# A decoder layer on one core: x's blocks summed on chip, low parts and scalings moved by a step, the gates started earlier

## The chip, the core and the metric

The kernel runs on one core of one Trainium2 chip. The metric is the device time of one execution in microseconds (us). A core has these engines, each with a queue of its own that it works off in order: TensorE (PE, matmuls; PEld is its weight load), VectorE (DVE), ScalarE (ACT), GpSimd (POOL) and SyncE (SP, which issues most DMAs). DMAs are issued from the queues of SP, ACT and POOL. An instruction that waits for a semaphore holds everything behind it on its engine.

## The reference, cut to what matters

```python
xn = rmsnorm(h, g_mix)                                   # x: 512 x 2048, float32
q_a, k_c, v_c, k_s, v_s, k_w, v_w, g_nsa, c_q, c_kv, k_r, gate_a, gate_b = split(xn @ w_in)
o_a = nsa_attention(...)                                 # compressed, selected and window branches
o_b = mla_attention(...)                                 # 16 heads, low-rank keys and values
mixed = sigmoid(gate_a) * (o_a @ w_o_nsa) + sigmoid(gate_b) * (o_b @ w_o_mla)
h = h + mixed @ w_out
h = h + memory_cross_attention(rmsnorm(h, g_xattn), rmsnorm(mem, g_mem), ...)   # 256 tokens of memory
h = h + square(relu(rmsnorm(h, g_mlp) @ w_ff1)) @ w_ff2
return rmsnorm(h, g_final)
```

All arrays are float32. There is one layer, a sequence of 512, a width of 2048, and an MLP of 8192.

## The kernel before, in words

**Matmuls in two parts.** Every operand of a matmul is split into a high part, rounded to the type that PE takes at full rate (ACT writes it: `copy` or `activation` with a scale), and a low part, the difference (DVE writes it: `tensor_sub`, or `scalar_tensor_tensor` with a scale). A product is three matmuls: high times high, high times low, low times high (`mm`, L516 to L518, for the attention's side; L2086 to L2088 for gates and MLP). `split` (L526 to L533) writes both parts at once. `split_late` (L546, L547 or L549, L550) writes the high part and puts the low part on a list that is worked off one or two runs later.

**Order of the work.** The schedule is written out by hand. A stage is a loop over chunks of columns; in a chunk, k runs over the blocks of 128 input features, and in each k the four blocks of 128 tokens (tt) get their three matmuls. Between the matmuls of a chunk other work is dealt out: weights (`Stream`: loads by SP at L320, high parts at L335, low parts at L347; the raw areas are two, and a load waits for the low part of the unit that lay in its area), attention (`side`, one piece at a time, at a rate given for each stage), and one background generator, `self.bg`, that is advanced once or four times per k (`bgn`). `on_k(k)` is called ahead of the matmuls of a k. PSUM banks come from rings: four `mm`, three `st` and one `o`; a transpose into `st` waits for the readers of the bank three allocations ago.

**Stages.** Seven projection chunks `P` (0 to 6) of xn @ w_in without its gates; two chunks `M` for MLA's low-rank inputs; memory's keys (`mem_k`) and values (`mem_v`) beside NSA's attention; for each quarter of MLA's heads its queries, keys and values (`mla_q`, `mla_kv`) and then a chunk `wn` of o_a @ w_o_nsa; the gates (`Gates.run`); the mix (`mix`, chunks `wm`); w_out; cross attention; the MLP.

**Seven products for eight.** Gates, w_out and MLP work on two-by-two blocks with seven block products, whose operands are sums of blocks. For the gates the blocks of x, scaled by g_mix, are `d_x[t, h, i]` in DRAM (t half of the tokens, h half of the features, i half of that half; 512 KB each), and the sums are `d_s[n, i]`, n from 1 to 4. `x_blocks` (L938 to L972) makes both. It starts at k = 13 of chunk 0 with four loads of x from DRAM (L947, SP), goes on as background in chunk 1, four steps per k, scales the four areas of 128 x 1024 in 16 steps on ACT (L960), stores them (L961), makes four sums on DVE (L968) and stores each (L969); then the same for i = 1, whose loads are issued ahead of the sums of i = 0. Sums 3 and 4 are written over the areas A[1, 1] and A[0, 1]. The same chunk 1 holds, from k = 4 on, `proj_post(0)`: rotations on POOL (`rope`, L635 to L638, after L1053 on DVE), then `to_compress` for each tt: four transposes into an `st` bank (L1112), two into another (L1120), copies by ACT (L1114, L1122) and low parts by DVE (L1115, L1123).

**Memory.** `mem_load` loads the 8 parts of mem, and in 16 steps splits them (ACT L532, DVE L533), squares and adds them (ACT L624, POOL L625). A step is taken in each k of chunk `M` 1, and then in each k under 15 of `mem_k(0)`; the rest is drained at k = 12. `mem_scale` multiplies memory's keys by their row's norm (a broadcast by two matmuls, ACT copy, DVE product L1733 of 128 x 1024) and scales the values (ACT L1736, two of 128 x 512). It stands between `mla_kv(2)` and chunk `wn` 1.

**Heads' rows.** `load_o` reads the eight stored pairs of heads back from DRAM and splits them (ACT L529, DVE L530), one per step, three steps after its load; once for NSA (in MLA's second quarter) and once for MLA (in the gates).

**Start of the gates.** In the last chunk `wn` 3 (8 values of k) the gates get ready. The generator `fetch` (four loads from d_x and d_s: L2326, L2331) runs as background: its first step does nothing, the second issues the loads, at k = 1. At k = 5 come four loads of weights (`loads(4)`, L1885), at k = 6 and 7 `ahead(0)` and `ahead(1)`. `ahead(s)` casts one half of the first moving operand (`stat`, ACT L1976), writes the low part of the half before (`stat_low`, DVE L1981), and calls `prep(s)`: high parts of weights up to s + 1 (ACT L1897), low parts up to s (DVE L1902), loads up to s + 4. Loads of the second and later products add the new weights to an area in place (POOL, L1892), so each waits for the two parts made of what lay in it. `Gates.run` then calls, for each product p and each j of 0 to 3, `prep(4p + j + 3)`, `stat` or `stat_low` for the next product, and the matmuls; at its very start it also calls `stat_low(0, 1)`.

## Time and profile before

| | |
|---|---|
| median of 3 runs | 2803.4 us (2802.63 to 2807.19) |
| profiled execution, its own time | 2804.49 us |
| its span | 2802.7 us |
| granted clock of PE, mean | 0.996 |
| DVE, ACT, POOL busy | 72%, 59%, 17% of the span |
| read from HBM, written | 460.84 MB, 50.33 MB |
| chunk P 0, P 1 (x's blocks) | about 5 to 50 us, 50 to 101 us |
| chunk M 1 (memory's loading), mem_k(0) | about 494 to 546 us, 546 to 560 us |
| chunk wn 3, gates | about 829 to 858 us, 858 to 1175 us |

The time of a kernel is taken in several executions; the profile is one more, with its own time. Its span runs from the first to the last instruction. In a row of the timeline stand the start (us), the duration (us), engine and line, operation, what it writes and reads with shapes, the count where several were merged, and in brackets the idle time of the engine just before it and what ended that. In the list of waits stand who waited for whom, us in total, times, and the longest. PE's matmuls overlap: a row's duration is longer than the distance to the next.

### The profile page before, as it was taken

How to read it: one execution, taken by the hardware profiler on the slowest of the kernel's cores; microseconds unless marked ns; L12 is line 12 of the kernel's file. 1: busy time of each engine (PE TensorE's matmuls, PEld its weight loads, DVE VectorE, ACT ScalarE, POOL GpSimd, SP SyncE). 2: the span in 40 equal slices, each digit the busy share in tenths (PEclk: the TensorE clock that was granted, in tenths of full speed). 3: DMA queues.
4: the chain of work that ended last, by engine and by line, in shares of the span. 5: the costliest groups of instructions: out<-in, count | busy, mean ns of one | idle time of the engine just before them, and what ended most of it. 6: DMA issues, size and time to landing. Idle time of an engine off the chain costs nothing.

```text
span 2802.7 us, 38326 instructions
## 1 busy us (share of the span) xinstructions
PE 2766.2 (99%) x13974; PEld 2354.6 (84%) x13974; DVE 2022.5 (72%) x3195; ACT 1645.5 (59%) x2746; POOL 467.6 (17%) x690
## 2 busy tenths in 40 slices
PE   9899999999999999999999999999999999999998
PEld 8788889888887788889998888888888888888887
DVE  6547766777666777657775877777777778888788
ACT  6435555776665666534566766766666644444445
POOL 3111111211111111101220111111111111111110
PEclk9999999999999999999999999999999999999999
DMA  7531111223338998879644988889888989889996
GB/s 247 196 97 59 67 56 65 95 100 106 106 136 225 259 232 188 265 263 228 154 95 152 241 207 208 204 221 216 210 216 200 235 225 228 225 227 235 239 232 174
DMA packets 171726, 513.69 MB, mean 183 GB/s; under 512 B 17552, under 2 KB 38928, under 8 KB 171536
## 3 DMA queue, kind: packets, MB, share of 16 engines
q0 software_dynamic: 50688, 184.57, 34.8%
q1 hardware_dynamic: 96064, 295.56, 30.0%
q10 hardware_dynamic: 24784, 31.11, 3.2%
q8 instruction: 109, 1.79, 0.3%
q14 instruction: 81, 0.66, 0.1%
HBM read 460.84 MB, written 50.33 MB: 182 GB/s over the span
## 4 chain that ended last, share of the span: by engine, by line
PE 81%; DMA 5%; DVE 5%; ACT 3%; issue 3%; POOL 1%; SPq 0%; DVEq 0%; POOLq 0%; ACTq 0%
PE mm L2087 10%; PE mm L2086 10%; PE mm L2088 10%; PE mm L516 7%; PE mm L517 7%; PE mm L518 7%; PE st L2086 5%; PE st L2088 5%; PE st L2087 5%; DMA s<-wts 4%; PE st L801 2%; PE o L820 1%; PE st L516 1%; PE mm L1656 1%; PE mm L1658 1%
## 5 line engine op out<-in xcount | busy, mean ns | idle before, releaser
L2086 PE MATMUL mm<-s,s 128*128 128x512 f32 x1472 | 575.0, 391 | 2.9 <-ACT s L2434 2.1
L2087 PE MATMUL mm<-s,s 128*128 128x512 f32 x1472 | 573.0, 389 | 0.1
L2088 PE MATMUL mm<-s,s 128*128 128x512 f32 x1472 | 572.9, 389 | 0.0
L1902 DVE TENSOR_TENSOR s<-s,s 128x1024 fp32r<-128x1024 f32 x307 | 372.7, 1222 | 201.2 <-ACT s L1897 200.4
L1897 ACT CAST s<-s 128x1024 fp32r<-128x1024 f32 x307 | 318.1, 1049 | 207.9 <-DMA s<-wts 160.1
L516 PE MATMUL mm<-s,s 128*128 128x512 f32 (+5 forms) x1044 | 411.7, 394 | 1.9 <-DVE s L1524 0.7
L518 PE MATMUL mm<-s,s 128*128 128x512 f32 (+5 forms) x1044 | 394.9, 378 | 0.2 <-DVE s L533 0.2
L517 PE MATMUL mm<-s,s 128*128 128x512 f32 (+5 forms) x1044 | 394.5, 378 | 0.0
L347 DVE TENSOR_TENSOR s<-s,s 128x512 fp32r<-128x512 f32 (+4 forms) x408 | 286.3, 717 | 90.1 <-ACT s L335 89.5
L335 ACT CAST s<-s 128x512 fp32r<-128x512 f32 (+4 forms) x408 | 242.1, 604 | 158.6 <-DMA s<-wts 81.9
L2086 PEld LDWEIGHTS mm<-s,s 128*128 128x128 f32 x1472 | 276.6, 188 | 60.7 <-ACT s L2434 2.5
L2088 PEld LDWEIGHTS mm<-s,s 128*128 128x128 f32 x1472 | 276.6, 188 | 57.5
L2087 PEld LDWEIGHTS mm<-s,s 128*128 128x128 f32 x1472 | 276.7, 188 | 56.9 <-DVE s L1902 0.5
L1897 ACT CAST s<-d 128x1024 fp32r<-128x1024 f32 x168 | 174.5, 1048 | 175.5 <-DMA d<-wts 148.6
L2086 PE MATMUL st<-s,s 128*128 128x512 f32 x676 | 264.2, 391 | 0.0
L2088 PE MATMUL st<-s,s 128*128 128x512 f32 x676 | 262.8, 389 | 0.0
L2087 PE MATMUL st<-s,s 128*128 128x512 f32 x676 | 262.5, 388 | 0.0
L1892 POOL DMA_DIRECT2D s<-wts x160 | 139.8, 876 | 714.1 <-DVE s L1902 330.5
L1902 DVE TENSOR_TENSOR s<-d,s 128x1024 fp32r<-128x1024 f32 x168 | 204.3, 1221 | 70.2 <-ACT s L1897 69.8
L518 PEld LDWEIGHTS mm<-s,s 128*128 128x128 f32 x1044 | 196.6, 188 | 34.5 <-DVE s L533 1.0
L704 ACT ACTIVATE PP<-PP,mx 128x512 f32<-128x512 f32 (+2 forms) x208 | 116.3, 559 | 184.7 <-DVE mx L703 184.2
L516 PEld LDWEIGHTS mm<-s,s 128*128 128x128 f32 x1044 | 197.3, 189 | 25.3 <-DVE d L1369 1.2
(393 smaller groups left out, 5090.8 us busy)
## 6 DMA issues: line engine op xcount, KB each, us to landing
s<-wts SPq DMA_DIRECT2D x278, 512.0 KB, 5.4
s<-wts POOLq DMA_DIRECT2D x192, 512.0 KB, 8.6
d<-wts POOLq DMA_DIRECT2D x108, 512.0 KB, 8.6
d<-wts SPq DMA_DIRECT2D x60, 512.0 KB, 8.1
PP<-wts POOLq DMA_DIRECT2D x52, 512.0 KB, 8.5
PP<-wts SPq DMA_DIRECT2D x33, 512.0 KB, 8.1
d_u<-s ACTq DMA_DIRECT2D x64, 256.0 KB, 5.3
d<-d_u SPq DMA_DIRECT2D x19, 512.0 KB, 8.4
```

The source lines that it names most:

```text
L335: self.k.nc.scalar.copy(o.hr, self.at[n][:, s])
L347: self.k.nc.vector.tensor_sub(o.lr, t[:, s], o.hi)
L516: t.matmul(ps, a.hr, b.hr, start=first, stop=False)
L517: t.matmul(ps, a.hr, b.lr, start=False, stop=False)
L518: t.matmul(ps, a.lr, b.hr, start=False, stop=last)
L704: self.later("x", 1, lambda: nc.scalar.activation(p, p, AF.Exp, bias=mx, scale=-1.0, accum_out=sm))
L1892: self.nc.gpsimd.dma_start(t, src, accum_op=OP.add)
L1897: self.nc.scalar.copy(t.hr, self.raw[i])
L1902: self.nc.vector.tensor_sub(t.lr, r, t.hi)
L2086: m(ps, a.hr, b.hr, start=first, stop=False, skip_group_check=True)
L2087: m(ps, a.hr, b.lr, start=False, stop=False, skip_group_check=True)
L2088: m(ps, a.lr, b.hr, start=False, stop=last, skip_group_check=True)
```

## The change

- `x_blocks` no longer loads x. The blocks are put together on DVE from the two parts that chunk 0 left on chip (`self.X[k]`, high + low, already scaled by g_mix): 32 additions of 128 x 256, two in a step. It starts with chunk 1. The block d_x[1, 0, i], which nothing reads, is not stored. The sums come in the order 1, 4, 2, 3, three steps apart instead of two; sum 4 is written over A[1, 0] instead of A[0, 1].
- `mem_load` writes a part's low part at the start of its next step, and `mem_k(0)` takes a step of it in every third k instead of every k.
- `load_o` likewise writes each low part a step later.
- `mem_scale` becomes a generator that is advanced once per k in the chunks of the mix, so it runs in k = 1 to 4 of the first of them.
- Start of the gates: `fetch` at k = 0, the four loads of weights at k = 1 (before: 5), `stat(0, 0)` at 3, `prep(0)` at 4, `stat_low(0, 0)` and `stat(0, 1)` at 5, `prep(1)` at 6, `stat_low(0, 1)` and `prep(2)` at 7 of chunk `wn` 3; `Gates.run` no longer begins with `stat_low(0, 1)`.

```diff
     def x_blocks(self):
         nc, v = self.nc, self.nc.vector
-
-        def load(i):
-            A = {}
+        for i in range(2):
+            A = {(t, h): self.slots.get() for h in range(2) for t in range(2)}
             for h in range(2):
-                for t in range(2):
-                    d = 8 * h + 4 * i
-                    A[t, h] = self.slots.get()
-                    nc.sync.dma_start(A[t, h].rearrange("p (k n) -> p k n", k=4),
-                                      self.a["xT"][d:d + 4, :, 256 * t:256 * t + 256].rearrange("k p n -> p k n"))
-            return A
-
-        A = load(0)
-        for i in range(2):
-            if i == 0:
-                yield
-            for h in range(2):
-                for t in range(2):
-                    for kk in range(4):
-                        yield
-                        x, d = A[t, h][:, 256 * kk:256 * kk + 256], G_MIX + 8 * h + 4 * i + kk
-                        nc.scalar.activation(x, x, AF.Copy, scale=self.gains[:, d:d + 1])
+                for kk in range(4):
+                    yield
+                    x = self.X[8 * h + 4 * i + kk]
+                    for t in range(2):
+                        s = slice(256 * t, 256 * t + 256)
+                        v.tensor_add(A[t, h][:, 256 * kk:256 * kk + 256], x.hi[:, s], x.lo[:, s])
+                for t in range(1 + h):
                     nc.sync.dma_start(self.d_x[t, h, i], A[t, h])
-            B = load(1) if i == 0 else None
             S = [self.slots.get(), self.slots.get()]
-            for n, o, f, a, b in ((1, S[0], v.tensor_sub, A[1, 0], A[1, 1]), (2, S[1], v.tensor_sub, S[0], A[0, 0]),
-                                  (3, A[1, 1], v.tensor_add, S[1], A[0, 1]), (4, A[0, 1], v.tensor_sub, A[0, 0], A[1, 0])):
+            for n, o, f, a, b in ((1, S[0], v.tensor_sub, A[1, 0], A[1, 1]), (4, A[1, 0], v.tensor_sub, A[0, 0], A[1, 0]),
+                                  (2, S[1], v.tensor_sub, S[0], A[0, 0]), (3, A[1, 1], v.tensor_add, S[1], A[0, 1])):
                 yield
                 yield
                 f(o, a, b)
                 nc.sync.dma_start(self.d_s[n, i], o)
+                yield
             yield
             self.put(*S, *A.values())
-            A = B
...
             if k == 8:
                 self.late_loads()
-            elif k == 13:
-                self.bg = self.x_blocks()
-                next(self.bg)
-                self.bg, self.xb = None, self.bg
...
-                self.bg, self.bgn = self.xb, 4
+                self.bg, self.bgn = self.x_blocks(), 4
...
-            if q == 2:
-                self.mem_scale()
             self.wn(q - 1, T["rw"], rows if q == 1 else None)
...
         g = Gates(self)
-        self.bg = g.fetch()
 
         def on_k(k):
             if k:
                 self.put(self.N[k - 1])
-            if k == 5:
-                drain(self.bg)
-                g.loads(4)
             if k == 6:
                 self.W.trim()
-            if k > 5:
-                g.ahead(k - 6)
-
+            steps[k]()
+
+        steps = [g.fetch, lambda: g.loads(4), lambda: None, lambda: g.stat(0, 0), lambda: g.prep(0),
+                 lambda: g.ahead(1), lambda: g.prep(1), lambda: (g.stat_low(0, 1), g.prep(2))]
         self.wn(3, T["rw"], on_k)
...
     def load_o(self, dram, out, lag=3):
...
-        for j in range(8 + lag):
+        low = None
+        for j in range(9 + lag):
+            if low:
+                h, x = low
+                self.nc.vector.tensor_sub(h.lr, x, h.hi)
+                out.append(h)
             if j < 8:
...
-            if j >= lag:
+            if lag <= j < 8 + lag:
                 while not self.slots.free:
                     yield
-                out.append(self.slot_hl())
-                self.split(out[-1], st[(j - lag) % 4])
-            yield
+                low = self.slot_hl(), st[(j - lag) % 4]
+                self.nc.scalar.copy(low[0].hr, low[1])
+                yield
+            elif j < lag:
+                yield
...
     def mix(self):
...
+        scale = self.mem_scale()
...
             def on_k(k):
+                next(scale, None)
...
     def mem_load(self):
...
-                self.split(h, x, self.gains[:, G_MEM + k:G_MEM + k + 1])
+                nc.scalar.activation(h.hr, x, AF.Copy, scale=g)
                 self.sumsq(x, k, sq[:, e * 256:e * 256 + 256], self.macc)
+                yield
+                nc.vector.scalar_tensor_tensor(h.lr, x, g, h.hi, op0=OP.mult, op1=OP.subtract)
                 self.MX.append(h)
-                yield
...
         def on0(k):
-            if k < 15:
+            if k % 3 == 0:
                 next(self.ml, None)
...
     def mem_scale(self):
         nc = self.nc
+        yield
         t = self.slots.get()
         rbm = t[:, :256]
         self.bcast(self.rm, rbm, 2)
+        yield
         k = self.kf.rearrange("p (h m) -> p h m", h=4)
         nc.vector.tensor_mul(k, k, rbm[:, None, :].to_broadcast([128, 4, 256]))
+        self.put(t)
         for i in range(2):
+            yield
             v = self.vf[:, i * 512:i * 512 + 512]
             nc.scalar.activation(v, v, AF.Copy, scale=self.rm[:, i:i + 1])
-        self.put(t)
...
     def ahead(self, step):
-        if step:
-            self.stat_low(0, step - 1)
+        self.stat_low(0, step - 1)
         self.stat(0, step)
-        self.prep(step)
...
-                if p == j == 0:
-                    self.stat_low(0, 1)
```

More of the change, by code (lines that the diff above doesn't have):

```diff
@@ L1446, in on_k @@
                 self.put(self.N[k - 1])
-            if k == 5:
-                drain(self.bg)
-                g.loads(4)
             if k == 6:
                 self.W.trim()
-            if k > 5:
-                g.ahead(k - 6)
+            steps[k]()
+        steps = [g.fetch, lambda: g.loads(4), lambda: None, lambda: g.stat(0, 0), lambda: g.prep(0),
+                 lambda: g.ahead(1), lambda: g.prep(1), lambda: (g.stat_low(0, 1), g.prep(2))]
         self.wn(3, T["rw"], on_k)
         self.put(self.N[-1])
-        self.bg = None
         return g
@@ L1684, in mem_load @@
                 k, x, s = 2 * j + e, st[j % 4][:, 256 * e:256 * e + 256], t[:, 512 * e:512 * e + 512]
-                h = HL(s[:, :256], s[:, 256:])
-                self.split(h, x, self.gains[:, G_MEM + k:G_MEM + k + 1])
+                h, g = HL(s[:, :256], s[:, 256:]), self.gains[:, G_MEM + k:G_MEM + k + 1]
+                nc.scalar.activation(h.hr, x, AF.Copy, scale=g)
                 self.sumsq(x, k, sq[:, e * 256:e * 256 + 256], self.macc)
+                yield
+                nc.vector.scalar_tensor_tensor(h.lr, x, g, h.hi, op0=OP.mult, op1=OP.subtract)
                 self.MX.append(h)
-                yield
         self.put(*sl[:2])
@@ L2318, in fetch @@
         self.A = {}
-        yield
         self.half(0, 0)
```

## Prediction

> **What bounds the kernel now.** I read the page first, then the list of waits of PE, then the timeline of every engine around each long wait, and at last a table of windows for the granted clock.
>
> ```profile
> PE 2766.2 (99%) x13974; PEld 2354.6 (84%) x13974; DVE 2022.5 (72%) x3195; ACT 1645.5 (59%) x2746; POOL 467.6 (17%) x690
> ```
>
> PE is busy for 2766.2 of 2802.7 us, so no edit that leaves the matmuls alone can bring more than the 36.5 us that are left, and what slow stretches hide inside the busy time. The other engines matter only where PE waits for them. The waits of PE, in us in total, times and longest:
>
> ```profile
> PE st L1120 <- DVE kc L1115: 6.4, 1, 6.4
> PE st L516 <- DVE s L547: 4.6, 5, 1.7
> PE o L822 <- DVE s L547: 4.2, 3, 2.4
> PE st L1300 <- DVE s L547: 2.4, 1, 2.4
> PE mm L2086 <- ACT s L2434: 2.1, 1, 2.1
> ```
>
> These five lines hold 19.7 us. Asked by stretches, the list puts them at 78 to 85 us (projection), 500 to 575 (memory's loading), 685 and 731 (MLA), 864 to 867 (start of the gates) and 955 (gates). From 1300 to 2750 us PE has no wait over 0.4 us, so that the MLP, half of the span, can only lose. The windows (PE, PEld, DVE, ACT and POOL busy us with instructions, granted clock, DMA share, GB/s) show what a wait costs beyond itself:
>
> ```profile
> 50.00:78.30 28.30, 28.30 (x148) 25.40 (x147) 12.59 (x21) 15.90 (x35) 8.72 (x17) 1.00 0.83 293
> 78.30:84.90 6.60, 0.20 (x2) 0.00 (x0) 1.09 (x2) 4.29 (x10) 0.00 (x0) 0.80 0.77 309
> 85.00:89.00 4.00, 4.00 (x12) 3.45 (x13) 2.90 (x5) 3.83 (x8) 0.00 (x0) 0.50 0.33 131
> 502.40:505.10 2.70, 0.33 (x3) 0.07 (x2) 1.08 (x3) 1.89 (x6) 0.67 (x1) 1.00 0.00 0
> 505.50:508.90 3.40, 3.40 (x16) 3.17 (x15) 2.85 (x9) 3.40 (x10) 0.47 (x1) 0.51 0.02 5
> 867.30:870.70 3.40, 3.20 (x9) 2.09 (x9) 0.00 (x0) 0.70 (x1) 0.47 (x1) 0.51 1.07 265
> 954.90:957.40 2.50, 0.40 (x2) 0.00 (x0) 1.54 (x2) 2.50 (x4) 0.86 (x1) 1.00 1.07 211
> ```
>
> After three of the stops (6.6, 2.7 and about 2.7 us) the clock was granted at half for some 3.4 us or more with PE back at work; after the fourth (2.1 us of idle) it stayed at 1.00. Half speed over 4 us loses 2.0 us, over 3.4 us up to 1.7. The Trainium skill (TensorE: Matmul & The Clock Gate, "HAM oscillation") says to avoid PE-idle gaps above about 3.4 us. Here a gap of 2.7 us was enough, and the row decides; by the page the two shorter stops would be worth their idle time alone.
>
> **Stage 1: x's blocks (second projection chunk).** Rows of ACT, DVE:
>
> ```profile
> 80.61 0.58 ACT L335 CAST s<-s 128x464 fp32r<-128x464 f32 x1 [7.04 <-DMA s<-wts]
> 81.10 1.70 ACT L960 ACTIVATE s<-s,gains 128x256 f32<-128x256 f32 x4
> 82.70 1.04 ACT L1114 CAST kc<-st 96x512 fp32r<-96x512 f32 x1
> 83.78 1.08 DVE L1115 TENSOR_TENSOR kc<-st,kc 96x512 fp32r<-96x512 f32 x1 [9.34 <-ACT kc L1114]
> 68.58 1.23 DVE L968 TENSOR_TENSOR s<-s,s 128x1024 f32<-128x1024 f32 x1 [1.18 <-DMA d_x<-s]
> 56.76 0.18 DVE L598 RECIPROCAL rs<-rs 128x4 f32<-128x4 f32 x1 [2.48 <-ACT rs L595]
> ```
>
> ACT stood 7.04 us on a load of weights; behind it in its queue lay four scalings (L960) and the first copy of the compression (L1114), whose PSUM bank PE wanted at 78.3. The weights were late for two reasons: DVE, whose low parts free their raw areas, had stood on a store of x (L968, because block sum 3 and 4 write over areas still being stored), and the DMA engines were at 0.83 with eight 512 KB loads of x among the traffic. The change removes these eight loads, two of eight stores, all 32 scalings on ACT, and the wait of sum 4; sum 3 comes eleven steps after its store instead of six. So the wait for weights should go. What is late next is DVE: the 32 additions are now its work. By 78.3 it must have done its 12.6 us of before, two more sums (six instead of four have been issued by then, 2.5 us), the copy's low part (1.1 us), and the additions. No row shows such an addition. The nearest is the 256-wide low part L533, with ACT's and POOL's beside it:
>
> ```profile
> 502.68 0.46 ACT L546 CAST s<-st 128x384 fp32r<-128x384 f32 x1
> 504.02 0.48 DVE L533 SCALAR_TENSOR_TENSOR s<-s,gains,s 128x256 fp32r<-128x256 f32 x1 [2.10 <-ACT s L532]
> 504.42 0.55 DVE L547 TENSOR_TENSOR s<-st,s 128x384 fp32r<-128x384 f32 x1
> 508.43 0.73 POOL L625 TENSOR_TENSOR s<-s 128x256 f32<-128x256 f32 x1 [3.27 <-ACT s L624]
> 508.49 0.95 DVE L533 SCALAR_TENSOR_TENSOR s<-s,gains,s 128x256 fp32r<-128x256 f32 x1
> ```
>
> It takes 0.48 us and lets the next one start after 0.40; beside POOL's L625 it took 0.95. At 0.40, 32 additions are 12.8 us. The sum is 12.6 + 2.5 + 1.1 + 12.8 = 29.0, and DVE's wait for the square root (2.5) stays: 31.5 us in a stretch of 28.3. DVE comes 3.2 us late, PE waits that long, and half a clock for 3.4 us adds up to 1.7: 4.9 us. Before, it was 6.4 + 2.0 = 8.4. **Term 1: -3.5 us.** Bounds: a quarter of L968's 1.23 for an addition (0.31) leaves DVE 0.3 late, -8.1; 0.95 for the sixteen additions of the second half, which run beside POOL's rotations (POOL was busy 8.7 of the 28.3 us), puts 8.8 us on top, +5.3. I take 0.40 since POOL is idle in the first half.
> The Trainium skill (SBUF — State Buffer, "Who interferes with whom") speaks against the move: a DVE instruction with two SBUF inputs and a GpSimd instruction that reads SBUF exclude each other, and ACT never waits for either. The pair 0.48 and 0.95 agrees; by that rule alone the stage would give the +5.3 of the first rival below.
>
> **Stage 2: low parts of memory.** At 502 DVE waited 2.10 us for ACT's high part of memory, with L547 behind it, ready since 503.1 (502.68 + 0.46), and PE behind that. With the low part of the step before in its place, L547 starts 1.3 us sooner; PE's 2.4 becomes 1.1, short of what halved the clock, which gives up to 1.7 more (I take 1.2: 16 matmuls passed in the 3.4 us). Two more places:
>
> ```profile
> 539.10 0.48 DVE L533 SCALAR_TENSOR_TENSOR s<-s,gains,s 128x256 fp32r<-128x256 f32 x1 [0.89 <-ACT s L532]
> 551.60 0.48 DVE L533 SCALAR_TENSOR_TENSOR s<-s,gains,s 128x256 fp32r<-128x256 f32 x1 [1.43 <-ACT s L532]
> 552.68 0.49 DVE L533 SCALAR_TENSOR_TENSOR s<-s,gains,s 128x256 fp32r<-128x256 f32 x1 [0.59 <-ACT s L532]
> ```
>
> The first is worth 0.9. At 551 three steps of the loader came in a row within the first three k-steps; with one in three the last of them is no longer in front of L547, 1.1. **Term 2: -4.5 us** (bounds -2 and -7). The steps still end at k = 9, before k = 15 needs the last part. The heads' rows have the same form, with DVE waits but only small ones of PE near: **-0.4** (0 to -1).
>
> **Stage 3: scaling of memory's keys and values.**
>
> ```profile
> 728.66 1.21 DVE L1733 TENSOR_TENSOR s<-s,s 128x1024 f32<-128x1024 f32 x1
> 731.00 0.38 PE L516 MATMUL st<-s,s 96*128 96x256 f32 x1 [1.01 <-DVE s L547]
> 1193.31 0.69 DVE L347 TENSOR_TENSOR s<-s,s 128x512 fp32r<-128x512 f32 x1 [2.07 <-ACT s L335]
> ```
>
> L1733 stood before L547, and PE waited 1.01 us. In its new place, the first chunk of the mix, its two small matmuls, ACT copies and DVE product (1.21) stand before gate work; DVE waits 2.07 us there for ACT, which covers it. Without that cover it costs 1.2. **Term 3: -1.0 us** (+0.2 to -1.0).
>
> **Stage 4: start of the gates.**
>
> ```profile
> 828.09 2.37 SPq L1885 DMA_DIRECT2D s<-wts  x4
> 849.94 1.04 ACT L1976 CAST s<-s 128x1024 fp32r<-128x1024 f32 x1
> 855.80 1.05 ACT L1976 CAST s<-s 128x1024 fp32r<-128x1024 f32 x1
> 857.20 1.22 DVE L1981 TENSOR_TENSOR s<-s,s 128x1024 fp32r<-128x1024 f32 x1
> ...
> 866.51 0.56 DVE L547 TENSOR_TENSOR s<-st,s 128x384 fp32r<-128x384 f32 x1
> 867.12 0.33 PE L822 MATMUL o<-s,d 128*128 128x128 f32 x1 [2.40 <-DVE s L547]
> 860.20 0.87 POOL L1892 DMA_DIRECT2D s<-wts  x1 [5.11 <-ACT s L1399]
> 870.00 1.04 ACT L1897 CAST s<-s 128x1024 fp32r<-128x1024 f32 x1 [6.19 <-DMA s<-wts]
> 871.47 0.44 PE L820 MATMUL o<-s,d 128*128 128x384 f32 x1 [0.97 <-ACT s L546]
> ```
>
> The first loads went out at 828.09, 22 us before the first cast: SP had run ahead, so moving them five steps earlier is worth nothing by itself and passes nothing on SP that waits. What counts are the casts. Seven low parts of 1.1 us stand on DVE between 857.20 and 866.51 before the L547 that PE waits for; four of them move into k-steps 5 to 7 of the chunk before, where L547 comes some 4.5 us sooner, before PE asks. The adding load of 860.20 took 9.8 us and held ACT 6.19 us; its low part moves one step ahead (steps are about 5 us here, 849.94 to 855.80), so it lands near 865 and holds ACT for about 1. Gone are 2.4, the half clock (1.0 for the five matmul gaps in it) and most of 0.97 plus what ACT adds there: **term 4: -4.4 us** (0 to -6). The stop at 955 comes under a DMA share of 1.07; PE arrives some 4 us sooner and three loads start about as much sooner: 0 (-2 to +2).
>
> **Sum:** -3.5 - 4.5 - 0.4 - 1.0 - 4.4 = -13.8. The profiled execution took 2804.5 us, so 2790.7; the median of the runs, 2803.4, lies 1.1 below it: **2789.6 us**.
>
> **Rivals.** (1) DVE becomes the bound of the second projection chunk: the additions exclude POOL's rotations; term 1 is +5.3. For: 0.95 beside POOL. Against: POOL is idle for two thirds of the stretch. -13.8 + 8.8 = -5.0: 2798.4. (2) The gates start no sooner, since the DMA engines (1.07) and not the casts set their pace and the stop at 955 takes up what 864 gives: term 4 is 0, or the edit does not do what it says, as its loads were early already. 2794.0. (3) Slower: in k-steps 3 to 7 of the chunk before the gates, six casts of 1.05 us now stand on ACT before the attention's copies, and wait for slots that PE has just read or for loads not landed; each such stop is a 2.4 us wait plus half a clock, 3.5 us. Term 4 gone (-9.4), five of the six blocked give +8: 2811.5. It decides from three blocked casts on. Against: ACT is not the last one before 857 in any wait of PE there.
>
> **How the numbers follow.** 0.2% (5.6 us) is about what a measurement of this kernel can tell. Forecast 0.62; rival 1 0.17, half of it on either side of -5.6; rival 2 0.13; both together (-0.6) 0.04; rival 3 0.04. Faster: 0.62 + 0.07 + 0.12 = 0.81; same 0.10 + 0.01 + 0.04 = 0.15; slower 0.04. The range goes from 2780 (term 1 at -8.1, terms 2 and 4 near their better bounds) to 2799.5, which takes in rivals 1 and 2.
>
> **What would show it.** PE's wait on L1115 gone or down to some 3 us, with DVE and not ACT as the late one (its row without a long idle time before it); no half clock at 505 and 868; DVE's wait for L532 gone from the list; no L1733 near 729; ACT's 6.19 us under 2. I am wrong if the wait on L1115 is as long as before, or if new waits stand between 829 and 858.

## The result, and the profile after

The changed kernel takes 2789.1 us (median of 4 runs, 2787.53 to 2790.86); the kernel before, on the same chip, 2804.9 us (4 runs, 2802.63 to 2807.19). The ratio is 0.9944, with a 95% interval of 0.9927 to 0.9961: faster by 15.8 us by the medians. The profiled execution took 2789.5 us with a span of 2787.7 us, 15.0 less than before. The prediction was 2789.6 us, within 2780 to 2799.5.

From the page of the changed kernel, PE's line, and the two queues of DMA that carry most (packets, MB, the time of their packets as a share of 16 engines' span):

```profile
PE 2762.4 (99%) x13974; PEld 2351.7 (84%) x13974; DVE 2033.4 (73%) x3227; ACT 1633.1 (59%) x2714; POOL 469.7 (17%) x690
...
q0 software_dynamic: 50688, 184.57, 35.1%
q1 hardware_dynamic: 91552, 290.32, 29.9%
```

PE still has 13974 matmuls, so the n-th of one trace can be set against the n-th of another, once the four that `mem_scale` takes to its new place (from 726 to 1163 us) are left out. PE's longest waits in the changed kernel:

```profile
PE mm L2077 <- ACT s L2420: 3.4, 1, 3.4
PE st L516 <- DVE s L547: 2.4, 5, 1.0
PE o L822 <- DVE s L547: 2.2, 3, 1.4
PE st L1104 <- DVE kc L1099: 1.6, 1, 1.6
```

Line numbers have moved: L1104 and L1099 are L1120 and L1115 of before, L2077 is L2086, L2420 (tanh of the gates) is L2434. The wait of 6.4 us in the second projection chunk is 1.6; the 2.4 us of memory's loading (L1300 on L547) is off the list; the 2.4 us at the start of the gates (L822) is 1.4. One wait has grown: the stop in the gates from 2.1 to 3.4 us. The windows (PE, PEld, DVE, ACT, POOL busy us with instructions, granted clock, DMA share, GB/s) at these places:

```profile
50.00:78.50 28.50, 28.50 (x147) 25.59 (x146) 25.29 (x56) 10.15 (x18) 8.24 (x12) 1.00 0.66 243
78.50:80.80 2.30, 0.69 (x6) 0.43 (x5) 2.27 (x3) 1.08 (x1) 2.14 (x5) 1.00 1.05 344
80.80:84.80 4.00, 3.88 (x22) 3.28 (x23) 3.92 (x5) 0.85 (x2) 0.21 (x2) 1.00 0.95 306
851.00:854.00 3.00, 1.65 (x12) 1.38 (x11) 2.97 (x6) 0.96 (x3) 0.87 (x1) 1.00 1.01 304
937.60:941.40 3.80, 0.38 (x2) 0.00 (x0) 1.53 (x2) 2.60 (x4) 0.86 (x1) 1.00 1.07 251
941.50:944.50 3.00, 3.00 (x7) 2.37 (x8) 1.62 (x2) 1.50 (x2) 0.89 (x1) 0.50 1.06 210
```

In the first stretch (50.00 to 78.30 before) DVE has gone from 12.59 to 25.29 us and ACT from 15.90 to 10.15. After the stop at 78.5 and the one at 851 the clock stays at 1.00, where before it was halved. After the stop at 937.6 it is halved, which before it was not.

Where the 14.4 us between the first and the last matmul came from: take the start of the same matmul in both traces, and ask how much their difference grows over a stretch. For example PE's row of the transposes at L1112 and the next at L1120 stood at 77.91 and 84.92 before; after (L1096, L1104) they stand at 78.51 and 80.71, so 7.01 us have become 2.20. In us, by the changed kernel's times, "before" less "after":

| stretch of the changed kernel | 0 to 45 | 45 to 120 | 120 to 490 | 490 to 600 | 600 to 760 | 760 to 846 | 846 to 880 | 880 to 920 | 920 to 946 | 946 to 1150 | 1150 to 1300 | to the end |
|---|---|---|---|---|---|---|---|---|---|---|---|---|
| what is there | chunk 0 | x's blocks | | memory | MLA, scaling | | gates' start | | gates' stop | | mix | |
| won | -0.6 | 7.0 | -0.1 | 4.2 | 1.8 | 0.7 | 4.2 | 0.2 | -2.9 | 0.0 | -0.1 | 0.2 |

### The profile page after: what moved, and what is told of

Its sections match the earlier page's. It is cut to its first block, busy times and chain, and to the rows that moved or that the text cites. A ratio compares the mean times of both kernels' runs of the same rounds, so it can differ in the third digit from the quotient of the medians.

```text
span 2787.7 us, 38302 instructions
## 1 busy us (share of the span) xinstructions
PE 2762.4 (99%) x13974; PEld 2351.7 (84%) x13974; DVE 2033.4 (73%) x3227; ACT 1633.1 (59%) x2714; POOL 469.7 (17%) x690
## 3 DMA queue, kind: packets, MB, share of 16 engines
q0 software_dynamic: 50688, 184.57, 35.1%
q1 hardware_dynamic: 91552, 290.32, 29.9%
## 4 chain that ended last, share of the span: by engine, by line
PE 83%; DMA 6%; DVE 5%; ACT 3%; issue 2%; SPq 0%; POOL 0%; DVEq 0%; POOLq 0%; ACTq 0%
PE mm L2077 10%; PE mm L2079 10%; PE mm L2078 10%; PE mm L516 7%; PE mm L518 7%; PE mm L517 7%; PE st L2079 5%; PE st L2077 5%; PE st L2078 5%; DMA s<-wts 2%; PE st L801 2%; DMA PP<-wts 1%; PE st L516 1%; PE st L518 1%; PE o L820 1%
## 5 line engine op out<-in xcount | busy, mean ns | idle before, releaser
L2077 PE MATMUL mm<-s,s 128*128 128x512 f32 x1472 | 575.0, 391 | 3.6 <-ACT s L2420 3.4
L2077 PEld LDWEIGHTS mm<-s,s 128*128 128x128 f32 x1472 | 276.7, 188 | 61.1 <-ACT s L2420 3.9
L2077 PE MATMUL st<-s,s 128*128 128x512 f32 x676 | 264.2, 391 | 0.0
```

Of the source, the lines that this page charges most:

```text
L2077: m(ps, a.hr, b.hr, start=first, stop=False, skip_group_check=True)
```

## The experiments

Each was timed in turn with the kernel before, which took 2803.3 us beside e1 to e4 and 2804.6 to 2804.9 beside the others and the change. The change itself was not timed again beside them. The first five take one part of the change away, or make it alone.

| run | median, us | ratio to before | 95% interval |
|---|---|---|---|
| the change | 2789.1 | 0.9944 | 0.9927 to 0.9961 |
| e1_old_xblocks | 2795.0 | 0.9972 | 0.9961 to 0.9982 |
| e2_old_memory | 2793.2 | 0.9959 | 0.9947 to 0.9972 |
| e3_old_gates_start | 2792.8 | 0.9962 | 0.9950 to 0.9975 |
| e4_old_scale | 2789.5 | 0.9951 | 0.9937 to 0.9965 |
| e5_only_xblocks | 2797.3 | 0.9973 | 0.9962 to 0.9983 |
| e6_sums_early | 2786.8 | 0.9936 | 0.9923 to 0.9948 |
| e7_pool_adds | 2789.7 | 0.9945 | 0.9932 to 0.9957 |
| e8_late_loads | 2787.2 | 0.9938 | 0.9926 to 0.9951 |
| e9_sums_later | 2788.1 | 0.9942 | 0.9928 to 0.9955 |
| e10_memory_rate | 2789.2 | 0.9947 | 0.9934 to 0.9959 |
| e11_gates_earlier | 2789.8 | 0.9950 | 0.9938 to 0.9963 |
| e12_both | 2784.0 | 0.9924 | 0.9910 to 0.9938 |

Executions of one kernel differ by 1.6 to 6.4 us, and the kernel before by 1.6 from one group of runs to another, so a part of 2 us can't be read from these medians. The same matmuls in the traces are sharper, as each stretch is compared by itself. Growth over a stretch against the changed kernel, positive where the variant loses time (columns as above):

| run | 0 to 45 | 45 to 120 | 490 to 600 | 600 to 760 | 760 to 846 | 846 to 880 | 880 to 920 | 920 to 946 | 1150 to 1300 | whole |
|---|---|---|---|---|---|---|---|---|---|---|
| e1_old_xblocks | -0.2 | 6.0 | 0.0 | 0.3 | -0.1 | -0.3 | -0.3 | -1.8 | -0.6 | 3.1 |
| e2_old_memory | 0.0 | 0.0 | 4.3 | 0.2 | -0.1 | -0.3 | -0.1 | -2.2 | 1.8 | 3.7 |
| e3_old_gates_start | -0.1 | 0.1 | -0.2 | 0.2 | 0.8 | 5.0 | -0.5 | -4.0 | 1.2 | 3.3 |
| e4_old_scale | 0.2 | 0.0 | 0.0 | 1.2 | -0.1 | -0.3 | 0.0 | -0.7 | 0.2 | -0.4 |
| e6_sums_early | -0.1 | 0.0 | -0.1 | 0.1 | -0.1 | -0.3 | -0.5 | -1.2 | -0.6 | -2.8 |
| e7_pool_adds | 0.6 | -0.2 | 0.2 | 0.1 | -0.1 | -0.3 | -0.1 | -0.9 | 1.1 | 0.2 |
| e8_late_loads | 0.9 | 0.2 | 0.1 | -0.1 | -0.1 | -0.3 | -0.5 | -1.8 | -0.6 | -3.2 |
| e9_sums_later | -0.8 | -2.1 | -0.1 | 0.1 | -0.1 | -0.3 | -0.4 | 1.3 | 0.2 | -1.6 |
| e10_memory_rate | -0.4 | 0.0 | 1.4 | 0.0 | -0.1 | -0.3 | -0.5 | 0.7 | -0.5 | -0.3 |
| e11_gates_earlier | 0.8 | 0.1 | -0.1 | -0.1 | 4.9 | -0.3 | -0.5 | -4.2 | -0.6 | -0.1 |
| e12_both | -1.0 | -2.2 | 0.1 | 0.1 | -0.1 | -0.1 | -0.5 | -1.3 | 0.4 | -5.5 |

No edit here touches the first 45 us, and there the runs lie within -1.0 and +0.9: such is the noise of one execution. The mix (1150 to 1300) varies more, from -0.6 to +1.8. The stop in the gates varies by itself too: e7, e8 and e10 leave what comes due at it as it was, PE reaches it within 0.1 us of the same time, and its wait is 2.8 to 3.2 us against the changed kernel's 3.4; and a half clock behind it, worth some 1.5 us in the column 920 to 946, comes or not (the last section says when).

**e1_old_xblocks**

```diff
-            A = {(t, h): self.slots.get() for h in range(2) for t in range(2)}
...
-                        v.tensor_add(A[t, h][:, 256 * kk:256 * kk + 256], x.hi[:, s], x.lo[:, s])
+                        nc.scalar.activation(x, x, AF.Copy, scale=self.gains[:, d:d + 1])
...
+            B = load(1) if i == 0 else None
```

> The changed kernel with the old making of x's blocks (eight loads of x, 32 scalings on ACT, the old order of the sums); everything else as changed. Theory (each part keeps the share that the start of the same matmul shows between the two traces: 7.0 us in the second projection chunk): 2789.1 + 7.0 = 2796 us, with PE's wait on L1115's counterpart back at about 6 us behind ACT's long wait for weights, and a half clock after it. Rival (the gates run at the pace of their DMAs, and what is won before 858 us is partly waited away at the stop near 938 us): the stop, 5.2 us with its half clock in the changed kernel, shrinks to about the 2.3 us of before, and the kernel takes about 2793 us.

Measured 2795.0 us, 5.9 over the changed kernel. Its waits of PE:

```profile
PE st L1120 <- DVE kc L1115: 5.2, 1, 5.2
PE mm L2093 <- ACT s L2436: 3.2, 1, 3.2
```

The stage loses 6.0 us, as the theory had it. The rival's reason for a smaller loss was wrong in its detail: the later stop did not shrink to 2.3 us, it is 3.2 long; but no half clock followed it, which gave most of the 1.8 back. PE reaches the stop 5.3 us later than in the changed kernel, and the cast on ACT that holds it starts 5.05 us later (943.85 against 938.80): the loads come later with PE, so what x's blocks win is not waited away there.

**e2_old_memory**

```diff
-                nc.scalar.activation(h.hr, x, AF.Copy, scale=g)
...
+                self.split(h, x, self.gains[:, G_MEM + k:G_MEM + k + 1])
...
-            if k % 3 == 0:
+            if k < 15:
```

> The changed kernel with memory's low parts written in the same step as the high parts again, and a step of the loader in each k under 15 of the keys. Theory: PE's wait near 502 us (2.4 us on DVE's low part, itself behind ACT's high part) and the half clock after it come back, 4.2 to 4.5 us by the start of the same matmul: 2793.5 us. Rival (the gates' stop near 938 us gives most of it back): about 2791 us, with the stop shorter by as much as the stage before it is longer.

Measured 2793.2 us, 4.1 over. The old wait is back word for word but for the line's number (L1284 is L1300 of before), and with it the half clock (0.83 granted on the mean from 498 to 508 us):

```profile
PE st L516 <- DVE s L547: 3.9, 5, 1.7
...
PE mm L2076 <- ACT s L2419: 2.8, 1, 2.8
PE st L1284 <- DVE s L547: 2.4, 1, 2.4
```

Its stage loses 4.3 us: 2.6 around this wait, 1.4 near 530 us, where PE waits 1.2 on L547 instead of 0.2, and 0.15 near 545. Here too 2.2 us come back at the gates' stop, some 1.5 of them because no half clock follows it and 0.6 by a shorter wait, which is no more than the stop varies; 1.8 are lost again in the mix.

**e3_old_gates_start**

```diff
+            if k == 5:
+                drain(self.bg)
+                g.loads(4)
...
-        steps = [g.fetch, lambda: g.loads(4), lambda: None, lambda: g.stat(0, 0), lambda: g.prep(0),
-                 lambda: g.ahead(1), lambda: g.prep(1), lambda: (g.stat_low(0, 1), g.prep(2))]
+            if k > 5:
+                g.ahead(k - 6)
```

> The changed kernel with the old start of the gates (loads of weights at k = 5, casts at k = 6 and 7, six low parts together). Theory (the start is worth 4.7 us, but 2.9 of it are given back at the stop near 938 us, since that stop's end is set by loads that do not start sooner by as much): 2789.1 + 1.8 = 2791 us, with the wait of 2.4 us near 850 us back and the stop of 938 us (3.4 us of waiting plus half a clock) back at 2.1 to 2.3 us without one. Rival 1 (the later stop is of its own, from the swapped order in the first product): the stop stays and the kernel takes 2793.8 us. Rival 2 (the gates run at the pace of the DMA engines): no difference, 2789 us.

```profile
PE o L822 <- DVE s L547: 3.2, 3, 2.4
...
PE mm L2081 <- ACT s L2429: 1.0, 1, 1.0
```

Measured 2792.8 us, 3.7 over. The start loses 5.0 us, and 0.8 ahead of it; then PE stands only 1.0 us at the later stop, without a half clock, and gets 4.0 of them back. So the later stop is not of its own: it takes up a good part of what the earlier start won, 2.4 us by the longer wait and some 1.5 by the half clock. Rival 1 falls as a mechanism, though its time, 2793.8, is nearer than the theory's 2791; in the trace the loss up to 946 us is 1.3 us net and the rest comes in the mix and behind it, which this edit doesn't touch. Rival 2 holds for most of the stretch, but not for the whole.

**e4_old_scale**

```diff
+            if q == 2:
+                self.mem_scale()
...
-                next(scale, None)
```

> The changed kernel with the scaling of memory's keys and values in its old place, ahead of the chunk of o_a @ w_o_nsa. Theory: L1733's counterpart stands before the late low part again, 0.45 us by the start of the same matmul: 2789.5 us, no difference that can be measured. Rival (its new place costs something near 1190 us that the trace of the changed kernel hides): the kernel becomes faster, about 2788.5 us. By the prediction's term it would be 2790.1 us.

Measured 2789.5 us. Its stage loses 1.2, of which some 0.45 is the own time of the four matmuls, which the changed kernel spends in the mix: about 0.7 net, between the theory's 0.45 and the prediction's 1.0. The whole can't be told from no change.

**e5_only_xblocks**

The kernel before with `x_blocks` of the change and its start in chunk 1, nothing else.

```diff
-            elif k == 13:
-                self.bg = self.x_blocks()
...
-                self.bg, self.bgn = self.xb, 4
+                self.bg, self.bgn = self.x_blocks(), 4
```

> The kernel before with the new making of x's blocks alone. Theory (the second projection chunk is worth 6.4 to 7.0 us and the loads of the gates shift with it, so that their stop near 955 us stays as it was): 2803.3 - 6.7 = 2796.6 us. Rival (the gates' stop gives back about 2 us by a half clock after it): 2798.6 us. By the prediction's term 1 alone it would be 2799.8 us.

```profile
PE mm L2070 <- ACT s L2418: 3.2, 1, 3.2
...
PE st L1104 <- DVE kc L1099: 1.7, 1, 1.7
```

Measured 2797.3 us, 7.6 under the kernel before and between theory and rival. The part gives alone what it gives among the others: in the trace 6.8 us in the second chunk. The gates' stop has grown from 2.1 to 3.2 us and has a half clock behind it, which takes 2.5 back in this execution (2798.2 us), as the rival has it, with nothing changed near the gates. That PE comes there sooner is not shown to be the cause: e1_old_xblocks and the changed kernel differ by the same part, and their stops are 3.2 and 3.4.

**e6_sums_early**

```diff
-        steps = [g.fetch, lambda: g.loads(4), lambda: None, lambda: g.stat(0, 0), lambda: g.prep(0),
+        steps = [g.fetch, lambda: g.loads(4), lambda: g.presum(2), lambda: g.stat(0, 0), lambda: g.prep(0),
...
-            if p < 3:
+            if 0 < p < 3:
                 self.presum(p + 2)
-            elif p < 5:
+            elif 2 < p < 5:
                 self.half(p - 3, 1)
```

> The changed kernel with the loads of the block sums for the third product (two of 512 KB) moved from the start of the first product to the idle step k = 2 of the chunk before, and the sums and blocks of the later products one product sooner too. Theory (the stop near 938 us is a backlog of the DMA engines, whose share is 1.04 to 1.07 from 850 to 950 us and 0.4 to 0.6 from 830 to 850 us): 1 MB of the backlog, about 3.5 us at the 300 GB/s of that stretch, moves to where the engines have room; the stop of 3.4 us and its half clock (1.6 us) go: about 2784 us, at least 2786 us. Rival (the chain of adding loads sets it, each waiting for two parts made from its area, or areas run short since the sums hold them longer): no gain, 2789 us, or up to 3 us slower by later loads of weights.

PE's longest wait in this kernel, and two of its windows (columns as above):

```profile
PE mm L2077 <- ACT s L2420: 2.4, 1, 2.4
```

```profile
820.00:830.00 10.00, 10.00 (x54) 8.47 (x54) 6.61 (x22) 6.12 (x13) 0.00 (x0) 1.00 1.00 403
830.00:840.00 10.00, 10.00 (x53) 8.52 (x53) 7.90 (x20) 6.76 (x15) 1.11 (x1) 1.00 0.39 82
```

Measured 2786.8 us, 2.4 under the changed kernel. The loads did move to 820 to 830 us, and the stop fell from 3.4 to 2.4 us, by 1.0 and not by 3.4. Less of the stop is a plain backlog than the theory had it. Against the 2.8 to 3.2 us of e7, e8 and e10, only 0.4 to 0.8 is gained; the comparison of e12_both with e9_sums_later shows the edit's effect more clearly. The half clock stayed.

**e7_pool_adds**

```diff
-                        v.tensor_add(A[t, h][:, 256 * kk:256 * kk + 256], x.hi[:, s], x.lo[:, s])
+                        (nc.gpsimd if t == 1 and i == 0 else v).tensor_add(A[t, h][:, 256 * kk:256 * kk + 256], x.hi[:, s], x.lo[:, s])
```

> The changed kernel with 8 of the 32 additions for x's blocks on POOL instead of DVE, in the first half, where POOL is idle. Theory (DVE is what comes late in the second projection chunk, by the 1.6 us that PE waits on L1099): DVE is free of 8 additions of 0.345 us, 2.8 us, the wait of 1.6 us goes, 2787.5 us. Rival (POOL's additions hold DVE off SBUF, so that what is taken from DVE comes back as longer instructions, and POOL starts its rotations later): wait as long as before or longer, 2789 to 2791 us.

Rows of POOL and DVE (start, us, engine, line; a duration over several merged instructions is their sum):

```profile
50.10 6.95 POOL L948 TENSOR_TENSOR s<-s 128x256 f32<-128x256 f32 x8
50.56 2.71 DVE L948 TENSOR_TENSOR s<-s 128x256 f32<-128x256 f32 x3
57.19 1.42 DVE L948 TENSOR_TENSOR s<-s 128x256 f32<-128x256 f32 x4
```

Measured 2789.7 us, no gain. Beside POOL's additions (0.87 us each) three of DVE's took 0.90 each; alone four took 0.36 each. PE's wait on L1099 went from 1.6 to 1.4. The rival holds for the instructions that run together. But DVE had room in this half of the stage anyway: what makes it late stands at the stage's end, as e9_sums_later shows.

**e8_late_loads**

```diff
-        steps = [g.fetch, lambda: g.loads(4), lambda: None, lambda: g.stat(0, 0), lambda: g.prep(0),
+        steps = [g.fetch, lambda: None, lambda: None, lambda: g.stat(0, 0), lambda: g.prep(0),
```

> The changed kernel with the gates' first loads of weights not issued at k = 1 but only when the first casts ask for them, at k = 4 of the chunk before. Theory (SP had run ahead, so the place of these loads in the program is worth nothing; the casts' place is): 2789 us, the loads still issued near 816 us. Rival (the earlier loads are what made the start sooner): the waits near 850 us come back, 2792 to 2794 us.

```profile
816.51 1.50 SPq L1876 DMA_DIRECT2D s<-wts  x2
818.53 1.60 SPq L1876 DMA_DIRECT2D d<-wts  x2
```

Measured 2787.2 us. The four loads went out at 816.5 to 820 us, with the first cast of these weights still some 13 us away (829.6): SP had run ahead. The place of these loads in the program is worth nothing. That this run is 1.9 us under the changed kernel comes, in the profiled execution, from the gates' stop: 3.2 us as in others, but with no half clock after it.

**e9_sums_later**

```diff
+            for _ in range(8 * i):
+                yield
             S = [self.slots.get(), self.slots.get()]
```

> The changed kernel with the four block sums of the second half put off by eight steps of the background (two k), so that two sums of 1.3 and 1.4 us no longer stand on DVE ahead of the first copy of the compression. Theory (DVE comes late there because of what is queued ahead of L1099, by 1.6 us): the wait on L1099 falls under 0.4 us, 2789.1 - 1.6 = 2787.5 us. Rival (DVE is short of time over the whole stretch, or ACT and the load of weights near 84 us are late next): another wait of 1 us or more comes within the same chunk, 2788.5 to 2790 us.

```profile
PE mm L2079 <- ACT s L2422: 4.0, 1, 4.0
```

Measured 2788.1 us. The wait on L1099 is gone from the list and the stage is 2.1 us shorter; the median, 1.0 under the changed kernel, can't show it. No other wait took its place in the chunk. The gates' stop is now the longest seen, 4.0 us, and takes 1.3 of it back.

**e10_memory_rate**

```diff
-            if k % 3 == 0:
+            if k < 15:
```

> The changed kernel with a step of memory's loader in each k under 15 of the keys again, the low parts still a step later. Theory by the prediction's terms (2.4 + 0.9 us from the low parts, 1.1 us from the rate): the waits of 545 to 552 us grow by 1.1 us in all, 2790.2 us. Rival (the low part in front of the copy was the whole matter, the rate is without effect): 2789.1 us.

A row of PE in this kernel, and DVE's two low parts ahead of it:

```profile
540.79 0.49 DVE L1676 SCALAR_TENSOR_TENSOR s<-s,gains,s 128x256 fp32r<-128x256 f32 x1 [1.43 <-ACT s L1673]
541.87 0.48 DVE L1676 SCALAR_TENSOR_TENSOR s<-s,gains,s 128x256 fp32r<-128x256 f32 x1 [0.59 <-ACT s L1673]
542.88 0.42 PE L516 MATMUL st<-d,s 96*128 96x320 f32 x1 [1.72 <-DVE s L547]
```

And two of its windows (columns as above):

```profile
541.10:544.52 3.42, 1.70 (x15) 1.64 (x14) 2.79 (x11) 3.42 (x14) 2.82 (x7) 1.00 0.03 7
544.52:547.93 3.41, 3.41 (x19) 3.41 (x17) 3.33 (x12) 3.28 (x15) 3.13 (x11) 0.50 0.35 115
```

Measured 2789.2 us: the median doesn't show it. The stage loses 1.4 us. The wait of before is back in its very form, two low parts waiting for their high parts in front of L547: 1.5 us more than in the changed kernel. But just behind it the changed kernel has 1.3 us of waits that this one hasn't (0.7 on L703, 0.4 on L1676, 0.2 on L547). What makes the 1.4 is the half clock, 1.3 us. In the kernel before and in e2_old_memory the same wait of 1.7 us had no half clock behind it, and this place costs them 0.15 us net. So the wait is what the theory said, but the rate by itself is worth next to nothing, as the rival has it, unless a half clock follows.

**e11_gates_earlier**

```diff
-        steps = [g.fetch, lambda: g.loads(4), lambda: None, lambda: g.stat(0, 0), lambda: g.prep(0),
...
+        steps = [lambda: (g.fetch(), g.loads(4)), lambda: g.stat(0, 0), lambda: g.prep(0), lambda: g.presum(2),
+                 lambda: g.ahead(1), lambda: g.prep(1), lambda: (g.stat_low(0, 1), g.prep(2)), lambda: g.prep(3)]
...
```

Not shown are the two lines of `Gates.run` that e6_sums_early changes; they are changed here too.

> The changed kernel with the sums' loads of e6_sums_early and the gates' casts and low parts one to two k sooner still (first casts of weights at k = 2 instead of 4, a fourth pair at k = 7). Theory (the stop near 938 us is the DMA engines' backlog, in which the adding loads pass at one in 3.9 us, and these loads begin only when the first low parts are made): the first adding load starts near 823 instead of 833 us, while the engines have room; the stop falls from 2.4 us of waiting in e6_sums_early to under 1 us, 2784 to 2785.5 us. Rival (the prediction's third: casts ahead of the attention's copies on ACT and low parts on DVE hold PE up between 829 and 858 us): two or more new waits there of 1 to 2.4 us, 2789 to 2793 us.

```profile
PE st L516 <- DVE s L547: 5.0, 8, 1.5
...
PE st L801 <- DVE mx L703: 1.2, 1, 1.2
PE mm L2077 <- ACT s L2420: 0.9, 1, 0.9
```

Measured 2789.8 us. Both mechanisms held, and the rival's time. The first adding load starts at 827.4 us instead of 832.9. PE has three more waits on L547 than in the changed kernel, 2.6 us more, and one on L703: 4.9 us lost between 760 and 846, where gate work now stands ahead of the attention's copies. The stop fell to 0.9 us, without a half clock, and 4.2 came back. Nothing is left.

**e12_both**

e6_sums_early and e9_sums_later together.

> The changed kernel with both edits that helped: the sums' loads of e6_sums_early and the later sums of e9_sums_later. Theory (each stage keeps its gain up to the start of the gates, 0.6 + 2.3 us, and the stop near 938 us lets through what its last weights allow): the two are not fully additive, since PE reaches the stop sooner by 2.3 us and part of that is waited away there: 2785.5 us. If they were additive: 2786.75 - 1.0 = 2785.8 us by the medians. Rival (the stop takes all of it back): 2787 us.

```profile
PE mm L2079 <- ACT s L2422: 2.2, 1, 2.2
```

Measured 2784.0 us (2781.55 to 2785.28), 5.1 under the changed kernel by the medians, 0.9924 of before (0.9910 to 0.9938): the best of all, and 1.5 better than the theory. The stop is 2.2 us, shorter than in either edit by itself. PE reaches it as early as in e9_sums_later (last matmul at 933.8 us in both) and leaves it 1.9 us sooner (936.35 against 938.26): that is what the sums' earlier loads are worth here. That the two together give more than their sum (5.1 against 2.4 + 1.0 by the medians, 5.5 against 2.8 + 1.6 in the traces) is not clear of the noise.

## Why the prediction was right, and where its parts were not

The total was right (13.8 forecast against 14.4 from matmul to matmul and 15.8 by the medians), but two terms were off by about 3 us, in opposite directions: x's blocks won 3.5 more than forecast, and the gates' stop, put at 0, took 2.9. That these two nearly cancel is luck.

**Term 1, x's blocks: right mechanism, wrong size (-3.5 forecast, -7.0 in the trace, -5.9 by taking it away, -7.6 by making it alone).** DVE did become the late engine and ACT's wait for weights went. Rows of DVE, POOL and PE in the changed kernel:

```profile
55.51 2.77 DVE L948 TENSOR_TENSOR s<-s 128x256 f32<-128x256 f32 x8
70.30 3.34 DVE L948 TENSOR_TENSOR s<-s 128x256 f32<-128x256 f32 x8
74.18 2.00 POOL L635 TENSOR_TENSOR rp<-s,cst 128x96 f32<-128x96 f32 x1 [2.16 <-DVE s L1037]
75.97 1.30 DVE L956 TENSOR_TENSOR s<-s,s 128x1024 f32<-128x1024 f32 x1
78.26 1.41 DVE L956 TENSOR_TENSOR s<-s,s 128x1024 f32<-128x1024 f32 x1
79.59 1.07 DVE L1099 TENSOR_TENSOR kc<-st,kc 96x512 fp32r<-96x512 f32 x1
80.71 0.41 PE L1104 MATMUL st<-cst,s 128*64 128x128 f32 x2 [1.61 <-DVE kc L1099]
```

L1099 has no idle time before it: DVE came to it late, behind L956. It cost PE 1.6 us, not the 3.2 worked out. The additions were priced well (0.35 alone, 0.42 in the second half, against 0.40). DVE was busy for 26.4 of the 29.6 us up to 79.59, so with L1099 27.5 where the prediction had 29.0, and idle for 3.2 where it had 2.5; and PE asked 0.6 us later than before (79.10 against 78.50), a lag of the first 45 us. So half of the miss of 1.6 us in the wait is less work on DVE, and the rest a later PE. As large a miss is the half clock: 1.7 us were charged for it, and after this stop there was none. Rival 1 did not come: DVE's 16 additions of the second half took 0.42 on the mean, 0.62 at most, and not 0.95, and the price fell on POOL, whose L635 took 2.00 us beside them (0.72 and 0.66 in the two rotations earlier), where nobody at that moment waited for it. The rule that was weighed there (the Trainium skill, SBUF — State Buffer, "Who interferes with whom") holds in e7_pool_adds, 0.90 against 0.36; what was wrong was to lay its cost on DVE.

**Term 2, memory: right in sum (-4.5 and -0.4 forecast; 4.2 in the trace, 4.1 by taking it away), not in each part.** The first low part with its half clock was put at 1.3 + 1.2 and won 2.6; the second, put at 0.9, won 1.4; the rate, put at 1.1, won 0.15, since the changed kernel waits elsewhere for nearly all that it saves there (e10_memory_rate). The heads' rows were not tried by themselves; the 1.8 us won from 600 to 760 less the 1.2 of e4_old_scale leave about 0.6 for them.

**Term 3, scaling: -1.0 forecast, about 0.7 net by the stage in e4_old_scale, nothing that the medians show.**

**Term 4, gates: the start right (-4.4 forecast, -4.9 in the trace from 760 to 880 us), the step after it wrong.** The prediction put the stop at 955 us at 0, because "three loads start about as much sooner". They did not, and the loss of 2.9 us lies outside the bounds of 2 given for it. Rows of POOL, ACT and PE in the changed kernel:

```profile
892.29 0.88 POOL L1883 DMA_DIRECT2D s<-wts  x1 [3.95 <-issue]
896.05 0.86 POOL L1883 DMA_DIRECT2D s<-wts  x1 [2.88 <-issue]
899.90 0.86 POOL L1883 DMA_DIRECT2D s<-wts  x1 [2.99 <-issue]
...
938.80 1.04 ACT L1888 CAST s<-s 128x1024 fp32r<-128x1024 f32 x1 [3.29 <-DMA s<-wts]
939.75 1.04 ACT L1967 CAST s<-s 128x1024 fp32r<-128x1024 f32 x1
940.69 1.26 ACT L2420 ACTIVATE s<-mm,hrx 128x512 f32<-128x512 f32 x2
941.42 0.76 PE L2077 MATMUL mm<-s,s 128*128 128x512 f32 x1 [3.44 <-ACT s L2420]
```

PE waits for a PSUM bank that the first tanh (half of the 1.26 us) still has to read; the tanh stands on ACT behind two casts, and the first of these waits 3.29 us for a load. The DMA engines are full from 850 on (1.01 to 1.07 in the windows), and POOL's adding loads go out one in 3.8 us there. So the last weights come at a time that depends on the DMA engines and not on PE alone: in e3_old_gates_start ACT's cast at this place starts 2.8 us later than in the changed kernel (941.59 against 938.80), while PE gets there 5.2 us later. The earlier start is thus worth about 2.8 us at this point and the rest is waited for; the half clock after it took up to 1.5 more in the profiled execution (seven matmuls at 0.43 us instead of 0.23). Rival 2 was half right, on the wrong half: the start did come sooner, and the stop then took up 2.9 of its 4.9 us. Taking the part away costs 3.7 us by the medians. One sign that the prediction named did not come: ACT's longest wait for a load here was to fall from 6.19 us to under 2, and it is 4.66 (before the cast at 856.97), but PE does not wait behind it.

Rival 3 did not happen in this change and does happen one to two k further on (e11_gates_earlier), in the form that DVE's L547 and ACT's copies come late, at 0.6 to 1.5 us a wait and without half a clock.

Left open: the tanh could be queued ahead of the cast that waits for a load, which would part PE from that load; it wasn't tried. Why e6_sums_early brought 1.0 us of the stop at most was not settled either.

## What to carry to other kernels

Price a removed wait together with what comes due right behind it: the gates' earlier start won about 5 us, and a stop 80 us further on, paced by loads, took 2.9 to 4.0 of them back, some 1.5 of that by a half clock. What x's blocks and memory won further ahead was kept, as the loads moved with PE. Relieve such a stop as well: with the sums' loads issued earlier PE left it 1.9 us sooner (e12_both against e9_sums_later). A queue is late where it is late: taking work off DVE at 50 us was worth nothing, moving two sums from 76 to after 80 us took the wait away.

## What the runs showed of the hardware

**The length of a stop does not tell whether the clock is halved after it; where it falls on a grid of 3.41 us does.** The stop in the gates, with its wait in us and the clock after it, in the profiled executions: 0.9 and 1.0 full, 2.1 full (before), 2.2 half, 2.4 half, 2.8 half (e7_pool_adds and e4_old_scale), 2.8 full (e2_old_memory), 3.1 half, 3.2 half (e5_only_xblocks), 3.2 full (e1_old_xblocks and e8_late_loads), 3.4 half, 4.0 half. The prediction charged each stop for half a clock by its length. But in every trace the granted clock changes only at times that are whole multiples of 3.413 us apart (in the changed kernel at 6.24, 941.49 and 944.90 us, 274 steps and one), and a half clock lasts one such step or two. Windows on this grid, of the changed kernel (two) and of e8_late_loads (three), columns as above:

```profile
938.08:941.49 3.41, 0.07 (x1) 0.07 (x1) 1.62 (x2) 2.69 (x4) 0.86 (x1) 1.00 1.08 249
941.49:944.90 3.41, 3.41 (x8) 2.71 (x9) 1.97 (x2) 1.50 (x2) 0.89 (x1) 0.50 1.05 210
...
936.18:939.60 3.42, 1.86 (x9) 1.21 (x7) 0.54 (x1) 1.00 (x2) 0.79 (x1) 1.00 1.06 282
939.60:943.01 3.41, 1.78 (x8) 1.48 (x9) 2.36 (x2) 2.99 (x5) 0.62 (x2) 1.00 1.08 220
943.01:946.42 3.41, 3.41 (x17) 2.83 (x16) 1.79 (x2) 1.86 (x3) 1.21 (x2) 1.00 1.03 241
```

The stop of 3.4 us leaves one window almost wholly idle, and the next is at half; the stop of 3.2 us is cut in two by the grid, with 1.56 and 1.63 us idle, and nothing follows. Over all fourteen traces, up to 2770 us, each of the 16 windows at full clock with 1.96 us or more of PE's idle time was followed by a half one, none with under 1.7, and of the four from 1.70 to 1.80 one (e10_memory_rate). The grid starts anew in each execution (the first change lies between 4.3 and 7.3 us), so for a stop of some 1.8 to 3.6 us (an estimate: once and twice the 1.8 us of idle time in one window) it is chance, worth about 1.5 us here. The Trainium skill (TensorE: Matmul & The Clock Gate, "HAM oscillation") sets the bound at some 3.4 us of idle PE; these rows show halving from 2.2 us on, and stops of 3.2 us without it. The same page's Part 1 calls the window in which activity is counted "free-running"; a grid that starts anew in each execution agrees with it.

**An adding load costs the DMA engines nearly twice a plain one.** By the page, q0 (POOL's adding loads) moved 184.57 MB in 35.1% of the engines' span, q1 290.32 MB in 29.9%: 0.190 against 0.103% for a MB, 1.85 times as much. q1 holds SP's loads and stores. No run separates the adding from the queue or from the sizes of the packets.
